# Keys and values of two kinds, projected 512 columns wide, four heads at a time

## The chip, the core and the metric

The kernel runs on one core of a Trainium2 chip. It computes one layer of a hybrid decoder, for 512 tokens of 1024 features, in one launch. The metric is the device time of an execution in microseconds (us). The engines are named as the profile names them: PE (matmul; PEld is its weight load), DVE (vector), ACT (scalar), POOL (GpSimd) and SP, whose queue issues most of the DMAs.

## What is computed

The layer is a feed-forward block, a mixer, a second feed-forward block and a gated embedding. The change is in the mixer, where one projection feeds two groups of heads. Cut to what matters here:

```python
a = rmsnorm(h, mix_norm[i])
u = a @ w_in[i]
(qa, kc, vc, ksl, vsl, kwn, vwn, ga, qf, kf, vf, fl) = jnp.split(u, split_points, axis=-1)
q_a = partial_rope(rmsnorm(split_heads(qa, N_HEADS_NSA), q_norm_nsa[i]), cos, sin)
...
k_slc = partial_rope(rmsnorm(split_heads(ksl, N_KV_NSA), k_norm_slc[i]), cos, sin)
k_win = partial_rope(rmsnorm(split_heads(kwn, N_KV_NSA), k_norm_win[i]), cos, sin)
...
o_a = nsa_attention(q_a, k_cmp, v_cmp, k_slc, split_heads(vsl, N_KV_NSA),
                    k_win, split_heads(vwn, N_KV_NSA), gates)
```

ksl, vsl, kwn and vwn are 128 columns each (two heads of 64): keys and values of the selected blocks (kind 0) and of the window (kind 1). They lie side by side in w_in, from column 768 on. Keys are normalized per head and the first 16 of their 64 features are rotated by position; values are used as they are.

## The kernel before

Tokens are handled in four tiles of 128 ("token 0" to "token 3" below, t in the code). Every float32 operand of a product is split into a part "hi" that is rounded to the matmul's type and a rest "lo", and a product is three matmuls: hi by hi, lo by hi, hi by lo (`passes`, L457). A tile of weights, 128 x 1024 numbers, is loaded on SP's queue into one of three buffers "st"; ACT copies it into one of four buffers "hi", and DVE subtracts that into one of four buffers "lo" (`split`, L373).

The stretch around the change is written in `mix` (L1068). `project` (L716) loads and splits its weights and then, for each token, issues 24 matmuls into one PSUM bank "acc" and calls `done`. First comes a projection "c" of 288 columns: the keys and values to be compressed ("T2"), gates and forget values. Then `kv_project(0)` and `kv_project(1)` (L1094), each 256 columns: for each token ACT scales the result out of PSUM into "u" (L1100), the values are split (L1102), the keys go through `head_norm` (L752: squares on ACT, a reduction on DVE, a scale and a power on POOL in `rstd`, two products on DVE), through `rope` on POOL (L742: four operations on tiles "r"), through `split_heads` (L769: a copy on ACT and a subtraction on DVE into "hl"), and PE transposes "hl" (L1109) so that copies can lay the keys into B. `q_project(0)` follows in the same manner, four heads wide.

Woven with it is the compression: `blocks` (L866) builds tiles from T2, for the keys on DVE and for the values on POOL, and `compressed` (L894) multiplies them with weights that are split tile by tile, eight matmuls a tile.

No one writes the order down. Each operation is recorded (`record`, L137) in the order in which `weave` (L197) takes the streams in turn, by the PE time that each has used. `issue` (L214) then orders all of them by a greedy rule: among the operations whose inputs are ready, on each engine, the one that by a table of costs can start first, within a window of 440 operations from the oldest that is left, and as far as the buffers of its tiles are free. Each engine executes its own list strictly in that order. So an edit at one place of the mixer moves operations up to the mixer's end.

Of the kernel before, what the change touches and what calls it, by code (L numbers as in the profile page):

```python
# [8 lines left out]
F32R = mybir.dt.float32r  # L9
AF = mybir.ActivationFunctionType  # L10
ALU = mybir.AluOpType
AX = mybir.AxisListType
PSUM = bass.MemoryType.PSUM

P = 128
# [13 lines left out]
NT = S // P  # L29
# [279 lines left out]
class Layer:  # L309
# [758 lines left out]
    def mix(self, xT, rs_in, o_nsa, o_fox, nsa_out):  # L1068
        nc = self.nc
        G, V = nc.gpsimd, nc.vector  # L1070
# [20 lines left out]
        nc.weave(self.project(xT, [(512, 256), (1280, 24), (2840, 8)], c_done, "c"))  # L1091
        B, Vt = {}, {}

        def kv_project(kind):  # L1094
            Vt[kind] = self.k4((P, 2, NT, P), F32R)
            B[kind] = [self.k4((P, 2, 512), F32R) for _ in range(2)]

            def kv_done(t, ps):
                u = self.w2()[:, :256]
                nc.scalar.mul(u, ps[:, :256], rs_in[t])  # L1100
                uv = u.rearrange("p (s h d) -> p s h d", s=2, h=2)
                self.vsplit(uv[:, 1], Vt[kind], t)  # L1102
                xn = self.w2()[:, :128].rearrange("p (h d) -> p h d", h=2)
                self.head_norm(V, uv[:, 0], xn, self.gkv[:, kind, None, :].to_broadcast([P, 2, 64]))
                self.rope(G, xn, t, 2)
                hl = self.split_heads(xn, 2, 2)
                tp = self.gub()
                for i in range(2):
                    nc.tensor.transpose(tp[:, i * P:(i + 1) * P], self.parts(hl, i, 0), self.ident)  # L1109
                k = tp[:, :256].rearrange("p (a c) -> p a c", a=2)  # L1110
                copy = nc.scalar.copy if t % 2 else V.tensor_copy
                cols = slice(t * P, (t + 1) * P)
                copy(B[kind][0][:, :, cols], k)
                copy(B[kind][1][0:64, :, cols], k[64:128])
                copy(B[kind][1][64:128, :, cols], k[0:64])
            yield from self.project(xT, [(768 + 256 * kind, 256)], kv_done, f"v{kind}")

        A = {}

        def q_project(g):  # L1120
            A[g] = [self.k4((P, 2, 512), F32R) for _ in range(2)]

            def q_done(t, ps):
                u = self.w2()[:, :256].rearrange("p (h d) -> p h d", h=4)
                nc.scalar.mul(u, ps[:, :256].rearrange("p (h d) -> p h d", h=4), rs_in[t])
                xn = self.w2()[:, :256].rearrange("p (h d) -> p h d", h=4)
                self.head_norm(V, u, xn, self.gq[:, None, :].to_broadcast([P, 4, 64]))
                self.rope(G, xn, t, 4)
                hl = self.split_heads(xn, 4, 2)
                for i in range(2):  # L1130
                    self.qT(hl, (2 * i, 2 * i + 1), A[g][i], t)
            yield from self.project(xT, [(256 * g, 256)], q_done, f"q{g}")

        def cmp_group(g):
            for t in range(NT):
                yield from self.cmp_attention(A[g], t, g, o_nsa)

        def nsa_pair(g, a):
            for kind in range(2):
                rs = self.rs_tile()  # L1140
                hd = 4 * g + 2 * a
                cols = slice(64 * hd, 64 * hd + 128)

                def write(ps, coef):
                    tmp = self.w2()
                    tv = tmp.rearrange("p (t h d) -> p t h d", t=NT, h=2)
                    V.tensor_mul(tv, ps, coef)
                    G.tensor_tensor(o_nsa[:, :, cols], o_nsa[:, :, cols],
                                    tmp.rearrange("p (t c) -> p t c", t=NT), ALU.add)
                run = lambda par: self.unit([(A[g][a][:, par], B[kind][i][:, g]) for i in range(2)], Vt[kind][:, g],  # L1150
                                            rs, par)
                yield from self.pair([run, run],
                                     rs, self.gates[:, :, hd:hd + 2, 1 + kind], write)
# [30 lines left out]
        def f_pair(p):  # L1184
# [7 lines left out]
            def write(ps, coef):  # L1192
                V.tensor_mul(o_fox[:, :, 128 * p:128 * p + 128].rearrange("p t (h d) -> p t h d", h=2), ps, coef)
            yield from self.pair([run, run], rs, None, write)

        chain = itertools.chain
        kv = kv_project(0)
        next(kv)
        wk = self.load_w1(self.d["cmp_k_w1"][0])
        blk = [self.blocks(T2[i], i) for i in range(2)]  # L1200
        cmp = chain(self.cmp_keys(blk[0], wk), self.cmp_values(blk[1], self.load_w1(self.d["cmp_v_w1"][0])),
                    self.forget_rows())
        nc.weave(chain(kv, kv_project(1), q_project(0)), cmp)
        streams = dict(c0=cmp_group(0), c1=cmp_group(1), n00=nsa_pair(0, 0), n01=nsa_pair(0, 1), n10=nsa_pair(1, 0),
                       n11=nsa_pair(1, 1), q1=q_project(1), out=nsa_out)
        for p in range(4):
# [336 lines left out]
```

## Time and profile before

| | |
|---|---|
| median of 3 runs | 1094.08 us (1092.9 to 1094.25) |
| the profiled execution | 1092.74 us |
| its span, first to last instruction | 1091.0 us |
| PE / DVE / ACT / POOL busy | 1070.5 / 768.9 / 580.0 / 192.9 us |
| granted TensorE clock, mean | 0.999 |

The profile is one execution. A busy engine is one on which an instruction runs; a matmul's end is modelled, and since matmuls are pipelined, the step from one start to the next tells more than a duration. Engine lists run in order, so an instruction that waits holds up all that stand behind it. All instructions have one line in the profile (L306, where the ordered list is emitted), and are told apart by the tiles that they write and read.

### The profile page before, as it was taken

What the parts mean: (1) busy time and instruction counts of PE and PEld (TensorE: products, weight loads), DVE (VectorE), ACT (ScalarE), POOL (GpSimd) and SP (SyncE); (2) the same over time, 40 slices, a digit from 0 to 9 for tenths busy, and PEclk for the clock granted to TensorE, in tenths of its full rate; (3) what the DMA queues carried; (4) which work ended last, traced back from release to release, by engine and by line L of the source; (5) the groups of instructions that cost most, each with busy time, mean ns of one, the idle gap of its engine ahead of it and who ended that gap; (6) DMA issues with size and microseconds to landing.
All of it is one profiled execution on the core that took longest, in us unless ns stands there. A gap on an engine that the chain in (4) does not pass through costs nothing.

```text
span 1091.0 us, 17966 instructions
## 1 busy us (share of the span) xinstructions
PE 1070.5 (98%) x6819; PEld 967.8 (89%) x6819; DVE 768.9 (70%) x1336; ACT 580.0 (53%) x1127; POOL 192.9 (18%) x338
## 2 busy tenths in 40 slices
PE   9999999999999989999999999999999999999998
PEld 6788899989997988899998888889989998899887
DVE  5976377835864777899889786977537874477473
ACT  5554155522543768888878864545414552255342
POOL 1010000000000366563344610310000000000000
PEclk9999999999999999999999999999999999999999
DMA  8486356733355521302102241677635664343431
GB/s 281 142 221 201 86 155 187 182 132 98 97 139 141 194 78 44 84 10 59 40 22 75 67 167 39 212 216 181 183 97 136 180 190 132 98 116 118 150 111 67
DMA packets 77446, 139.82 MB, mean 128 GB/s; under 512 B 13616, under 2 KB 35648, under 8 KB 77104
## 3 DMA queue, kind: packets, MB, share of 16 engines
q1 hardware_dynamic: 72400, 120.76, 34.1%
q0 software_dynamic: 4960, 17.91, 9.3%
q8 instruction: 54, 0.88, 0.3%
q14 instruction: 32, 0.26, 0.1%
HBM read 132.23 MB, written 6.42 MB: 127 GB/s over the span
## 4 chain that ended last, share of the span: by engine, by line
PE 82%; DVE 5%; POOL 3%; ACT 3%; issue 3%; DMA 3%; SPq 0%; ACTq 0%; POOLq 0%; DVEq 0%
PE acc L306 52%; PE gub L306 30%; DVE k L306 1%; DVE w L306 1%; POOL w L306 1%; POOL s L306 1%; DVE lo L306 1%; ACT w L306 1%; DMA pt<-in_quarters 1%; ACT k L306 1%; ACT hi L306 1%; POOL r L306 1%; DMA gq<-in_q_norm_nsa 1%; DMA st<-in_quarters 0%; DVE pt L306 0%
## 5 line engine op out<-in xcount | busy, mean ns | idle before, releaser
L306 PE MATMUL acc<-hi,k 128*128 128x512 f32 (+1 forms) x832 | 262.7, 389 | 2.7 <-DVE k L306 1.9
L306 ACT CAST hi<-st 128x1024 fp32r<-128x1024 f32 (+4 forms) x150 | 148.2, 991 | 181.4 <-PE acc L306 92.4
L306 DVE TENSOR_TENSOR lo<-st,hi 128x1024 fp32r<-128x1024 f32 (+4 forms) x150 | 172.9, 1155 | 64.2 <-ACT hi L306 64.1
L306 PE MATMUL acc<-hi,x 128*128 128x256 f32 (+3 forms) x784 | 203.2, 335 | 0.0
L306 PEld LDWEIGHTS acc<-hi,k 128*128 128x128 f32 x832 | 156.0, 188 | 33.9 <-issue 1.5
L306 PE MATMUL acc<-lo,k 128*128 128x512 f32 (+1 forms) x432 | 164.2, 383 | 0.2 <-DVE lo L306 0.2
L306 ACT CAST hi<-pt 128x1024 fp32r<-128x1024 f32 x68 | 71.3, 1049 | 159.1 <-PE acc L306 90.3
L306 PE MATMUL gub<-x,hi 128*128 128x256 f32 x816 | 147.4, 282 | 0.0
L306 PE MATMUL acc<-x,hi 128*128 128x256 f32 x816 | 147.3, 282 | 0.0
L306 PEld LDWEIGHTS acc<-hi,x 128*128 128x128 f32 x784 | 134.9, 189 | 8.2
L306 PE MATMUL gub<-k,hi 128*128 128x512 f32 (+1 forms) x560 | 138.3, 338 | 1.3 <-ACT hi L306 1.3
L306 DVE TENSOR_TENSOR lo<-pt,hi 128x1024 fp32r<-128x1024 f32 x68 | 83.1, 1223 | 78.8 <-ACT hi L306 78.8
L306 PE MATMUL acc<-lo,x 128*128 128x256 f32 (+3 forms) x392 | 130.8, 335 | 0.0
L306 PEld LDWEIGHTS gub<-x,hi 128*128 128x128 f32 x816 | 126.1, 189 | 0.7 <-DVE w L306 0.3
L306 PEld LDWEIGHTS acc<-x,hi 128*128 128x128 f32 x816 | 125.6, 188 | 0.0
L306 PE MATMUL gub<-x,lo 128*128 128x256 f32 x408 | 115.3, 283 | 0.0
L306 PE MATMUL acc<-x,lo 128*128 128x256 f32 x408 | 115.3, 283 | 0.0
L306 POOL DMA_DIRECT2D pt<-in_quarters x34 | 29.9, 879 | 477.4 <-DMA pt<-in_quarters 242.7
L306 PEld LDWEIGHTS gub<-k,hi 128*128 128x128 f32 x560 | 96.3, 190 | 12.9 <-ACT hi L306 1.8
L306 PE MATMUL gub<-k,lo 128*128 128x512 f32 (+1 forms) x280 | 94.5, 338 | 0.4 <-DVE lo L306 0.4
L306 PEld LDWEIGHTS acc<-lo,k 128*128 128x128 f32 (+1 forms) x432 | 79.5, 184 | 14.8 <-DVE lo L306 0.4
L306 PEld LDWEIGHTS acc<-lo,x 128*128 128x128 f32 x392 | 74.0, 189 | 4.5
(163 smaller groups left out, 1732.2 us busy)
## 6 DMA issues: line engine op xcount, KB each, us to landing
st<-in_quarters SPq DMA_DIRECT2D x51, 512.0 KB, 3.7
st<-in_ffn_wd SPq DMA_DIRECT2D x44, 512.0 KB, 5.0
pt<-in_quarters SPq DMA_DIRECT2D x34, 512.0 KB, 4.7
pt<-in_quarters POOLq DMA_DIRECT2D x34, 512.0 KB, 6.7
st<-in_quarters SPq DMA_DIRECT2D x32, 256.0 KB, 5.5
st<-in_w_in SPq DMA_DIRECT2D x48, 128.0 KB, 2.6
st<-in_first SPq DMA_DIRECT2D x16, 256.0 KB, 3.5
st<-in_w_in SPq DMA_DIRECT2D x8, 512.0 KB, 3.8
```

The source lines that it names most:

```text
L306: getattr(getattr(self.nc, op.eng), m)(*a, **k)
```

## The change

One call of `kv_project` takes the place of two. It projects 512 columns at once, so a token has one bank of 512 columns in the place of two of 256, and 24 matmuls in the place of 48. The four key heads of both kinds are squared, reduced, scaled, multiplied by their gains, rotated and split in one pass. The values are split kind by kind, and the transposes and the copies into B are made kind by kind, as before. A weight tile holds two slices of 128 rows by 512 columns where it held four by 256, so there are four tiles either way, but one token reads all four.

```diff
-        def kv_project(kind):
-            Vt[kind] = self.k4((P, 2, NT, P), F32R)
-            B[kind] = [self.k4((P, 2, 512), F32R) for _ in range(2)]
+        def kv_project():
+            for kind in range(2):
+                Vt[kind] = self.k4((P, 2, NT, P), F32R)
+                B[kind] = [self.k4((P, 2, 512), F32R) for _ in range(2)]
 
             def kv_done(t, ps):
-                u = self.w2()[:, :256]
-                nc.scalar.mul(u, ps[:, :256], rs_in[t])
-                uv = u.rearrange("p (s h d) -> p s h d", s=2, h=2)
-                self.vsplit(uv[:, 1], Vt[kind], t)
-                xn = self.w2()[:, :128].rearrange("p (h d) -> p h d", h=2)
-                self.head_norm(V, uv[:, 0], xn, self.gkv[:, kind, None, :].to_broadcast([P, 2, 64]))
-                self.rope(G, xn, t, 2)
-                hl = self.split_heads(xn, 2, 2)
-                tp = self.gub()
-                for i in range(2):
-                    nc.tensor.transpose(tp[:, i * P:(i + 1) * P], self.parts(hl, i, 0), self.ident)
-                k = tp[:, :256].rearrange("p (a c) -> p a c", a=2)
-                copy = nc.scalar.copy if t % 2 else V.tensor_copy
+                u = self.w2()
+                nc.scalar.mul(u, ps, rs_in[t])
+                uv = u.rearrange("p (a s h d) -> p a s h d", a=2, s=2, h=2)
+                for kind in range(2):
+                    self.vsplit(uv[:, kind, 1], Vt[kind], t)
+                xn = self.w2()[:, :256]
+                x4 = xn.rearrange("p (a h d) -> p a h d", a=2, h=2)
+                sq, ss = self.w2()[:, :256], self.small(4)
+                nc.scalar.activation(sq.rearrange("p (a h d) -> p a h d", a=2, h=2), uv[:, :, 0], AF.Square)
+                V.tensor_reduce(ss, sq.rearrange("p (n d) -> p n d", n=4), axis=AX.X, op=ALU.add)
+                r = self.rstd(ss, 64, 4).rearrange("p (a h) -> p a h", a=2)
+                V.tensor_tensor(x4, uv[:, :, 0], r[:, :, :, None].to_broadcast([P, 2, 2, 64]), ALU.mult)
+                V.tensor_tensor(x4, x4, self.gkv[:, :, None, :].to_broadcast([P, 2, 2, 64]), ALU.mult)
+                xn = xn.rearrange("p (n d) -> p n d", n=4)
+                self.rope(G, xn, t, 4)
+                hl = self.split_heads(xn, 4, 2)
                 cols = slice(t * P, (t + 1) * P)
...
-            yield from self.project(xT, [(768 + 256 * kind, 256)], kv_done, f"v{kind}")
+                for kind in range(2):
+                    tp = self.gub()
+                    for i in range(2):
+                        nc.tensor.transpose(tp[:, i * P:(i + 1) * P], self.parts(hl, 2 * kind + i, 0), self.ident)
...
+            yield from self.project(xT, [(768, 512)], kv_done, "v")
...
-        kv = kv_project(0)
+        kv = kv_project()
...
-        nc.weave(chain(kv, kv_project(1), q_project(0)), cmp)
+        nc.weave(chain(kv, q_project(0)), cmp)
```

The order moves with it. On DVE, around the first token's chain, before (w_630 is its "u", w_631 its normalized keys, k_618 to k_623 are the blocks and their parts):

```order
L306 TENSOR_REDUCE s_633<-w_632 128x2
L306 TENSOR_TENSOR k_618<-k_576,pos 128x16x31
L306 COPY k_577<-gub 64x2x128
L306 TENSOR_TENSOR k_618<-k_576,pos 128x16x31
L306 TENSOR_TENSOR k_619<-k_618,k_619 128x8x64
L306 TENSOR_TENSOR w_631<-w_630,s_634 128x128
L306 TENSOR_TENSOR w_631<-w_631,gkv 128x128
L306 TENSOR_TENSOR k_620<-k_618,k_620 128x8x64
```

The same place now (w_639 is token 0's "u", w_640 its normalized keys, k_627 to k_632 are the blocks and their parts, k_577 is filled just ahead):

```order
L306 TENSOR_TENSOR k_627<-k_576,pos 128x16x31
L306 TENSOR_TENSOR k_628<-k_627,k_628 128x8x64
L306 TENSOR_TENSOR k_629<-k_627,k_629 128x8x64
L306 TENSOR_TENSOR k_631<-k_630,k_631 128x8x64
L306 TENSOR_REDUCE s_642<-w_641 128x4
L306 TENSOR_TENSOR k_632<-k_630,k_632 128x8x64
L306 TENSOR_TENSOR k_607<-w_639,k_607 128x2x64
L306 TENSOR_TENSOR k_610<-w_639,k_610 128x2x64
L306 TENSOR_TENSOR w_640<-w_639,s_643 128x256
L306 TENSOR_TENSOR w_640<-w_640,gkv 128x256
```

The reduction stood ahead of the blocks' additions and now stands behind an addition and three of the four subtractions.

On ACT, from token 2's scaling on, before (w_652 is token 2's "u" of kind 0, w_662 token 3's; x_617 holds the last two of the four weight tiles of the compressed keys, the first two are copied before the first token's scaling):

```order
L306 ACTIVATE w_652<-acc,s_553 128x256
L306 CAST k_607<-w_652 128x2x64
L306 ACTIVATE w_654<-w_652 128x128
L306 CAST hi<-x_617 128x1024 x2
L306 ACTIVATE w_662<-acc,s_558 128x256
```

The same place now (w_665 is token 2's "u", x_625 and x_626 hold the four weight tiles of the compressed keys, "hi<-st" is the first tile of the queries):

```order
L306 ACTIVATE w_665<-acc,s_553 128x512
L306 CAST hl<-w_653 128x4x64
L306 CAST k_607<-w_665 128x2x64
L306 CAST k_610<-w_665 128x2x64
L306 CAST hi<-x_625 128x1024
L306 CAST k_608<-gub 128x2x128
L306 CAST k_609<-gub 64x2x128 x2
L306 ACTIVATE w_667<-w_665 128x256
L306 CAST hi<-x_625 128x1024
L306 CAST hi<-x_626 128x1024 x2
L306 CAST hi<-st 128x1024
L306 ACTIVATE w_678<-acc,s_558 128x512
```

All four tiles of the compressed keys' weights are now copied after token 2's scaling; two of them were copied before token 0's.

On PE, near the mixer's end, before (x_574 is the output of the first group of heads, "hl" is token 2 of the last projection of the forgetting heads, k_1577 and k_1578 are operands of the output projection):

```order
L306 MATMUL gub<-ident,x_574 128x128 x4
L306 MATMUL gub<-k_1488,k_1486 128x256
L306 MATMUL gub<-k_1489,k_1487 128x256
L306 MATMUL gub<-ident,x_574 128x128 x2
L306 MATMUL gub<-ident,hl 128x128 x2
L306 MATMUL acc<-hi,k_1577 128x512
L306 MATMUL acc<-lo,k_1577 128x512
```

The last of the rows between "gub<-ident,x_574" and the same "hl" now, where the six rows of 128x512 ahead of these are left out:

```order
L306 MATMUL gub<-ident,x_574 128x128 x4
L306 MATMUL acc<-hi,k_1541 128x512
L306 MATMUL gub<-ident,x_574 128x128 x2
L306 MATMUL acc<-lo,k_1541 128x512
L306 MATMUL acc<-hi,k_1542 128x512
L306 MATMUL gub<-ident,hl 128x128 x2
L306 MATMUL acc<-hi,k_1543 128x512
```

The transposes of "hl" stood ahead of the output projection's matmuls and now stand behind nine of them.

## Rows read from the trace of the kernel before

**Rows 1.** The page, part 1: busy us (share) and instructions of each engine.

```profile
PE 1070.5 (98%) x6819; PEld 967.8 (89%) x6819; DVE 768.9 (70%) x1336; ACT 580.0 (53%) x1127; POOL 192.9 (18%) x338
```

**Rows 2.** Windows: length, busy us (instructions) by engine, granted clock, DMA share, GB/s.

```profile
373.00:440.00 67.00, 60.33 (x493) 57.53 (x491) 52.65 (x133) 49.64 (x117) 42.68 (x93) 1.00 0.29 84
440.00:580.00 140.00, 138.56 (x927) 128.06 (x926) 125.77 (x385) 119.59 (x353) 60.45 (x101) 1.00 0.15 37
580.00:640.00 60.00, 56.27 (x347) 49.37 (x346) 49.59 (x134) 48.15 (x137) 29.56 (x41) 1.00 0.31 105
```

**Rows 3.** Timeline, PE: start, us, operation, tiles, shapes, count; every third matmul shown.

```profile
334.54 0.39 PE L306 MATMUL acc<-lo,k 128*128 128x512 f32 x1
...
344.74 0.39 PE L306 MATMUL acc<-lo,k 128*128 128x512 f32 x1
...
373.29 0.27 PE L306 MATMUL acc<-lo,x 128*128 128x256 f32 x1
...
376.43 0.29 PE L306 MATMUL acc<-lo,x 128*128 128x256 f32 x1
...
380.75 0.29 PE L306 MATMUL acc<-lo,x 128*128 128x256 f32 x1
```

**Rows 4.** Waits of PE, 373 to 421 us: waiter <- releaser: us, times, longest.

```profile
PE gub L306 <- DVE hl L306: 2.9, 4, 1.1
PE acc L306 <- DVE k L306: 1.3, 1, 1.3
PE gub L306 <- POOL w L306: 0.4, 1, 0.4
PE acc L306 <- DVE lo L306: 0.2, 1, 0.2
```

**Rows 5.** Groups by form, 373 to 440 us: count | busy us, mean ns | idle before.

```profile
L306 DVE TENSOR_TENSOR lo<-x,hi 128x1024 fp32r<-128x1024 f32 x8 | 9.8, 1230 | 0.6 <-ACT hi L306 0.4
L306 DVE TENSOR_TENSOR k<-k,k 128x512 fp32r<-128x512 f32 x4 | 3.8, 957 | 0.0
L306 DVE TENSOR_TENSOR hl<-w,hl 128x128 fp32r<-128x128 f32 x8 | 2.3, 291 | 5.2 <-ACT hl L306 5.1
L306 DVE TENSOR_TENSOR hl<-w,hl 128x256 fp32r<-128x256 f32 x4 | 1.6, 426 | 0.7 <-ACT hl L306 0.7
...
L306 ACT CAST hi<-x 128x1024 fp32r<-128x1024 f32 x8 | 8.3, 1046 | 0.2 <-PE acc L306 0.2
L306 ACT CAST hl<-w 128x256 fp32r<-128x256 f32 x4 | 1.5, 400 | 2.3 <-POOL w L306 2.3
...
L306 POOL TENSOR_TENSOR s<-s,mhalf 128x4 f32<-128x4 f32 x4 | 4.1, 1026 | 0.2
L306 POOL TENSOR_SCALAR s<-s 128x4 f32<-128x4 f32 x4 | 0.9, 220 | 1.8 <-DVE s L306 1.6
```

**Rows 6.** Timeline, DVE and POOL: the blocks of T2, and one rotation.

```profile
379.34 0.42 DVE L306 COPY k<-gub 64x256 f32<-64x256 f32 x1
379.79 1.03 DVE L306 TENSOR_TENSOR k<-k,pos 128x496 f32<-128x496 f32 x1
380.74 1.74 DVE L306 TENSOR_TENSOR k<-k,k 128x512 fp32r<-128x512 f32 x1
382.40 1.37 DVE L306 TENSOR_TENSOR w<-w,s 128x128 f32<-128x128 f32 x1
...
380.15 3.46 POOL L306 TENSOR_TENSOR k<-k,pos 128x496 f32<-128x496 f32 x2
...
428.68 0.32 POOL L306 TENSOR_TENSOR r<-w,cos 128x64 f32<-128x64 f32 x1 [1.10 <-DVE w L306]
428.96 0.46 POOL L306 TENSOR_TENSOR r<-w,sin 128x32 f32<-128x32 f32 x2
```

**Rows 7.** Timeline, PE, 620 to 625 us: the two that waited.

```profile
621.66 0.44 PE L306 MATMUL gub<-ident,x 128*128 128x128 f32 x2 [0.90 <-DVE s L306]
623.50 0.44 PE L306 MATMUL gub<-ident,hl 128*128 128x128 f32 x2 [1.40 <-DVE hl L306]
```

More of the change, by code (lines that the diff above doesn't have):

```diff
@@ L1092, in mix @@
         B, Vt = {}, {}
-        def kv_project(kind):
-            Vt[kind] = self.k4((P, 2, NT, P), F32R)
-            B[kind] = [self.k4((P, 2, 512), F32R) for _ in range(2)]
+        def kv_project():
+            for kind in range(2):
+                Vt[kind] = self.k4((P, 2, NT, P), F32R)
+                B[kind] = [self.k4((P, 2, 512), F32R) for _ in range(2)]
             def kv_done(t, ps):
-                u = self.w2()[:, :256]
-                nc.scalar.mul(u, ps[:, :256], rs_in[t])
-                uv = u.rearrange("p (s h d) -> p s h d", s=2, h=2)
-                self.vsplit(uv[:, 1], Vt[kind], t)
-                xn = self.w2()[:, :128].rearrange("p (h d) -> p h d", h=2)
-                self.head_norm(V, uv[:, 0], xn, self.gkv[:, kind, None, :].to_broadcast([P, 2, 64]))
-                self.rope(G, xn, t, 2)
-                hl = self.split_heads(xn, 2, 2)
-                tp = self.gub()
-                for i in range(2):
-                    nc.tensor.transpose(tp[:, i * P:(i + 1) * P], self.parts(hl, i, 0), self.ident)
-                k = tp[:, :256].rearrange("p (a c) -> p a c", a=2)
-                copy = nc.scalar.copy if t % 2 else V.tensor_copy
-                cols = slice(t * P, (t + 1) * P)
-                copy(B[kind][0][:, :, cols], k)
-                copy(B[kind][1][0:64, :, cols], k[64:128])
-                copy(B[kind][1][64:128, :, cols], k[0:64])
-            yield from self.project(xT, [(768 + 256 * kind, 256)], kv_done, f"v{kind}")
@@ new lines, in kv_done @@
+                cols = slice(t * P, (t + 1) * P)
+                for kind in range(2):
+                    tp = self.gub()
+                    for i in range(2):
+                        nc.tensor.transpose(tp[:, i * P:(i + 1) * P], self.parts(hl, 2 * kind + i, 0), self.ident)
+                    k = tp[:, :256].rearrange("p (a c) -> p a c", a=2)
+                    copy = nc.scalar.copy if (t + kind) % 2 else V.tensor_copy
+                    copy(B[kind][0][:, :, cols], k)
+                    copy(B[kind][1][0:64, :, cols], k[64:128])
+                    copy(B[kind][1][64:128, :, cols], k[0:64])
```

## The prediction

> **What bounds the kernel now.** I read the page first: the span is 1091.0 us and PE is busy for 98% of it, DVE for 70%, ACT for 53%, POOL for 18% [rows 1]. The profiled execution took 1092.74 us, so 1.74 us lie outside the span; the median of the three runs is 1094.08 us, 1.34 us above the profiled one. I form the sum on the profiled execution and carry its result over to the median.
>
> The windows by stage come next [rows 2]. [...] The change touches the second window, 373 to 440 us: PE is idle there for 67.00 - 60.33 = 6.67 us, a third of all its idle time. From 440 to 580 us it is idle for 1.44 us in 140, and from 580 to 640 us for 3.73 us. The reader should see that DVE is at 90% from 440 to 580 us and yet PE hardly waits: PE's own work is the bound there, and the others are cover that just suffices. So an edit counts by two things alone: what it takes from PE's work, and what it does to PE's waits.
>
> Third, PE's timeline gives the step from one matmul to the next [rows 3]: 45 matmuls of 512 columns in 344.74 - 334.54 = 10.20 us are 0.2267 us each; 36 of 256 columns in 380.75 - 376.43 = 4.32 us are 0.1200 us each. Fourth, PE's waits up to the last transposes of this projection [rows 4]: 2.9 + 1.3 + 0.4 + 0.2 = 4.8 us. The largest group, four waits of together 2.9 us, is the transposes of a token waiting for "hl", the end of the chain of normalization and rotation.
>
> **The change part by part.** *Matmuls.* Two kinds x 4 tokens x 24 matmuls of 256 columns become 4 x 24 of 512: 192 x 0.1200 - 96 x 0.2267 = 23.04 - 21.76 = 1.28 us less. They stand on the engine that bounds, so I take -1.28 us. [...]
>
> *The waits of the chains.* Eight chains of two heads become four of four heads, and each is longer. The 128x256 forms of the chain stand in the same window, from the query projection [rows 5]: the last subtraction takes 0.43 us (0.29 for two heads), the copy before it 0.40, the power on POOL 1.03. I take 0.43 us for the reduction and each of the two products too, which have the same shape on the same engine. The scaling of 512 columns out of PSUM has no row in this stage; it lies between the copies of 256 (0.40) and 1024 columns (1.05 [rows 5]), some 0.6 us, and beside other work for token 0. What matters is the work the order puts on PE over each chain.
>
> Token 0: the projection starts at about 373.17 us (its second matmul is at 373.29 [rows 3]); 24 x 0.2267 = 5.44 us, four transposes of "c" (0.4) and the wait of 0.4 us for their input, which stays [rows 4], end its matmuls at 379.4. The new order has 35 matmuls between them and its transposes, so PE arrives at 379.4 + 35 x 0.2267 = 387.3 us. The chain is bound elsewhere: in DVE's new order its reduction stands behind all work on the blocks but one piece. That starts when the last copy ahead of it ends, 379.76 us [rows 6]: one addition (1.03 [rows 6]), three subtractions (0.96 each [rows 5]) and the reduction (0.43) reach 384.1; scale and power on POOL (0.22 + 1.03 [rows 5]), the two products (0.86), the rotation on POOL (0.32 + 0.46 + 0.32 [rows 6]; the addition taken as long as the first product), copy and subtraction (0.40 + 0.43) reach 388.1, and eight hand-overs, estimated at 0.05 us each, 388.6. PE waits 1.3 us; between 0.8 (the copy 0.5 us earlier, since no reduction stands among the blocks' work any more) and 2.1 (1.3 + 1.74 - 0.96, one more subtraction held up by POOL, next).
>
> POOL's additions are slow company: while two of them take 3.46 us, a 128x512 subtraction of DVE takes 1.74 us where the mean is 0.96, and a 128x128 product 1.37 us [rows 5, 6]. [...]
>
> Tokens 1 to 3: token 1 has 33 wide matmuls over its chain and both transposes of token 0, and I find no wait. Token 2 has 24 wide ones, the 32 of the compressed keys and 28 of the queries, 24 x 0.2267 + 60 x 0.12 = 12.6 us, against a chain of about 6 us by the steps above, but on ACT and DVE its copy and its product stand behind the splits below: 1.2 us, between 0 and 1.7. Token 3: 0.3.
>
> *The splits of the compressing weights.* This is what the change costs. "hi" and "lo" have four buffers. The projection now needs four weight tiles for one token and holds all four until its last token has read them; before, two of the four "hi" copies of the compressed keys' weights ran in the first token's time. In the new order all four, and the first of the queries' weights, stand after token 2's scaling on ACT. Token 1's transposes come at 388.6 + 0.4 + 22 x 0.2267 = 394.0 us, the first tile is copied then (1.05 [rows 5]), and from about 395 us on DVE has five subtractions of 1.23 us [rows 5], three copies (3 x 0.42 [rows 6] = 1.3), a reduction and a product in a row: 5 x 1.23 + 1.3 + 0.43 + 0.43 = 8.3 us. PE has 15 wide matmuls and the 32 of the compressed keys for that time, 3.4 + 3.8 = 7.2 us. With 0.3 us by which DVE starts later and 0.6 in which it waits for a buffer to come free I take 2.0 us of waits, between 1.4 and 2.6. The waits of 1.3 and 0.2 us that belong to these matmuls now [rows 4] go.
>
> Together: 0.4 + 1.3 + 1.2 + 0.3 + 2.0 = 5.2 us in the place of 4.8, so +0.4; the ends are 0.4 + 0.8 + 1.4 = 2.6 (-2.2) and 0.4 + 2.1 + 1.7 + 0.3 + 2.6 = 7.1 (+2.3).
>
> *The rest of the mixer.* The planner orders everything anew up to the end of the mixer, about 640 us. One place can be priced: token 2 of the last forgetting projection now makes PE wait 1.40 us for its "hl" [rows 7]. In the new order nine matmuls of 512 columns, 2.0 us, stand ahead of these transposes, so that wait is covered. The 0.90 us just before it [rows 7] stands between the same rows in both orders and stays. Since the same reordering can open a wait of this size at any of the other chains, I count half of it, -0.7, between -1.4 and +1.0.
>
> *At no price.* The four loads of weight tiles stay four, and no load is among PE's releasers [rows 4]. The copies into B, the transposes, the table loads and the banks are the same in number or fewer.
>
> Sum: -1.28 + 0.4 - 0.7 = -1.6 us. 1092.74 - 1.6 = 1091.1 for a profiled execution, and 1094.08 - 1.6 = **1092.5 us** for the median. Its own range, with the terms half way to their ends, is 1091.0 to 1094.5 us.
>
> **The rivals.** *A, the chains are covered.* Half as many chains run through POOL and DVE, so both are freer than before and no chain is late: the low end of the waits and all of the 1.40: -1.28 - 2.2 - 1.4 = -4.9, 1089.2 us. For it: 2.9 us of today's waits are on "hl". Against it: token 0's reduction stands behind the blocks' work.
>
> *B, slower: the splits become the bound.* If each of the four tiles shows its copy and its subtraction (1.05 + 1.23 us [rows 5]) against the eight matmuls of 0.12 us that read it, PE waits 4 x (2.28 - 0.96) = 5.3 us instead of 2.0, and with tokens 0, 2 and 3 at their upper ends the waits are 0.4 + 2.1 + 1.7 + 0.3 + 5.3 = 9.8, +5.0; with the matmuls' -1.28 that is +3.7, 1097.8 us. It turns into a loss beyond what can be told from no change once the waits up to the last transposes pass 4.8 + 1.28 + 2.2 = 8.3 us. For it: these tiles wait for buffers that the wide projection holds. Against it: wide matmuls stand between the tiles' uses.
>
> *C, the freed vector work counts.* If DVE set the pace from 440 us on, each of 16 pairs of 128x128 instructions that becomes one of 128x256 gives 2 x 0.291 - 0.426 = 0.16 us [rows 5], 2.5 us, beside the matmuls: -3.8, 1090.3 us. For it: DVE's 90%. Against it: PE's 1.44 us of idle time in 140.
>
> **How the numbers follow.** About 0.2%, 2.2 us, is what a measurement of this kernel can tell from no change. My forecast, a gain too small for that, gets 0.44; A 0.27 and C 0.07 are faster by more; B 0.22 is slower by more. The range reaches to A's 1089.2 and B's 1097.8 with a little off the far end: 1088.8 to 1097.4 us. [...]
>
> **What would show it.** In the profile after: 96 matmuls of 512 columns of this projection with a step of 0.227 us; waits of PE on "hl" at token 0 of about 1.3 us and none at token 1; PE held by "lo" among the compressing matmuls between 395 and 405 us for about 2 us; busy time of PE lower by about 1.3 us; no wait at the nine wide matmuls of the last projection. Wrong would be: waits in this stage above 8 us (B) or below 3 us (A), or a wait of over 2 us at a chain that I did not look at, between 440 and 640 us.

## The result, and the profile after

The changed kernel takes 1085.95 us (median; 1085.05 to 1086.81), the kernel before 1094.11 us timed beside it: a ratio of 0.993, interval 0.9919 to 0.9942, so 8.2 us less. The prediction was 1092.5 us, between 1088.8 and 1097.4; it is wrong in the size and in the case that it held likeliest.

The page of the kernel after, part 1 (as [rows 1]):

```profile
PE 1068.3 (98%) x6723; PEld 963.0 (89%) x6723; DVE 767.7 (71%) x1320; ACT 579.4 (53%) x1115; POOL 183.6 (17%) x314
```

The span is 1085.0 us, 6.0 less. This profile reaches the mixer 1.2 us later than that of before, and is as much behind already at 75 us, where nothing has changed (in the profiles of this study the last matmul of "c" starts anywhere between 371.4 and 375.5 us). So 7.2 us were gained from there on, and the windows that answer to [rows 2] are moved by 1.2 us (columns as there):

```profile
374.20:441.20 67.00, 61.81 (x413) 54.23 (x412) 54.81 (x132) 50.94 (x120) 37.59 (x73) 1.00 0.30 86
441.20:581.20 140.00, 139.39 (x938) 130.27 (x937) 125.72 (x379) 120.20 (x348) 62.59 (x102) 1.00 0.16 39
581.20:641.20 60.00, 58.27 (x359) 51.46 (x358) 52.54 (x136) 50.17 (x136) 23.40 (x36) 1.00 0.33 115
```

PE is idle for 5.19, 0.61 and 1.73 us, where it was 6.67, 1.44 and 3.73. More than half of the idle time that went lies in the two later windows, where no line of the program was edited.

For the comparisons below I lay the lists of matmuls side by side by the work in them. A matmul of N columns counts 0.4167 N + 13.5 ns, an estimate laid through the two steps of [rows 3]: 226.7 - 120.0 = 106.7 ns for 256 columns more, and some 13 ns beside. At 128 columns or fewer it counts 60 ns, a choice of mine that no row shows (two of 128 columns take 0.38 us at 595.15 us where one takes 0.27 at 597.61, so a second one adds 0.11; timeline of the kernel before, PE); both kernels have the same 720 of these. What PE takes beyond this count is lost. "Stage" is the loss from the last matmuls of "c" to about 479 us, "later" from there to about 658 us, both against the kernel before. In this account the changed kernel has 1.3 us less work, loses 2.1 us less in the stage and 3.6 us less later: 7.0 of the 7.2 us. After 658 us the two lose the same. Since the lists differ in order, the split depends on where it is drawn: at 470, 500 or 520 us in the place of 479 the changed kernel's stage reads -2.4, -1.7 and -2.3, so it is good to some 0.4 us. And it is an account of one profiled execution a kernel, where the ratios below are of all executions.

### The profile page after: what moved, and what is told of

Read it like the earlier page. It is cut to its first block, busy times and chain, and to the rows that moved or that the text cites. A ratio compares the mean times of both kernels' runs of the same rounds, so it can differ in the third digit from the quotient of the medians.

```text
span 1085.0 us, 17692 instructions
## 1 busy us (share of the span) xinstructions
PE 1068.3 (98%) x6723; PEld 963.0 (89%) x6723; DVE 767.7 (71%) x1320; ACT 579.4 (53%) x1115; POOL 183.6 (17%) x314
## 4 chain that ended last, share of the span: by engine, by line
PE 82%; DVE 6%; ACT 3%; DMA 3%; POOL 3%; issue 3%; SPq 0%; ACTq 0%; POOLq 0%; DVEq 0%
PE acc L306 52%; PE gub L306 30%; DVE k L306 2%; DVE lo L306 2%; POOL s L306 1%; ACT k L306 1%; DVE w L306 1%; ACT w L306 1%; DMA pt<-in_quarters 1%; DMA k<-in_x 1%; POOL r L306 1%; DMA gq<-in_q_norm_nsa 1%; POOL w L306 1%; ACT hi L306 1%; DVE pt L306 0%
## 5 line engine op out<-in xcount | busy, mean ns | idle before, releaser
L306 PE MATMUL acc<-hi,x 128*128 128x384 f32 (+3 forms) x720 | 199.4, 349 | 0.3 <-ACT hi L306 0.3
L306 PEld LDWEIGHTS acc<-hi,x 128*128 128x128 f32 x720 | 127.1, 189 | 11.1 <-ACT hi L306 0.4
L306 PE MATMUL acc<-lo,x 128*128 128x384 f32 (+3 forms) x360 | 125.1, 348 | 1.7 <-DVE lo L306 1.7
L306 PEld LDWEIGHTS gub<-k,hi 128*128 128x128 f32 x560 | 96.3, 189 | 12.6 <-ACT hi L306 1.6
L306 PEld LDWEIGHTS gub<-x,lo 128*128 128x128 f32 x408 | 76.9, 188 | 0.0
```

Source lines behind the costliest of these rows:

```text
L306: getattr(getattr(self.nc, op.eng), m)(*a, **k)
```

## The experiments

Three theories stood at the start. "Fewer chains": four long chains in the place of eight are what helps. "Width": the wide matmuls are. "Order": the edit makes the planner order the rest of the mixer anew, and that order happens to be a better one. Each ratio is to the kernel before, timed on the same chip beside it; "work", "stage" and "later" are us against the kernel before, less is faster.

| kernel | work | stage | later | ratio |
|---|---|---|---|---|
| changed | -1.3 | -2.1 | -3.6 | 0.9930 |
| e1, wide bank, eight chains | -1.3 | +5.1 | -3.2 | 1.0003 |
| e2, narrow banks, four chains | 0 | -2.6 | -1.5 | 0.9968 |
| e3, before, all delays 204 ns | 0 | -0.5 | -2.9 | 0.9965 |
| e5, changed, later order of before | -1.3 | +2.1 | +1.0 | 1.0013 |
| e6, before, later order of changed | 0 | +3.6 | -3.7 | 0.9988 |

### One part of the change alone

*e1*: the bank is 512 wide, but each kind has its own scaling, norm, rotation and "hl", as before.

```diff
             def kv_done(t, ps):
+                for kind in range(2):
+                    u = self.w2()[:, :256]
+                    nc.scalar.mul(u, ps[:, 256 * kind:256 * kind + 256], rs_in[t])
...
             yield from self.project(xT, [(768, 512)], kv_done, "v")
```

> The change's projection of 512 columns, but each kind keeps its own chain of two heads (eight chains, as before). Theory 'fewer chains' (the gain of 8.2 us is 1.3 us of matmul work and the rest is that four chains take the place of eight): 1.3 us below before, some 1092.8 us, with PE's waits on hl back near the 7.0 us of before. Theory 'order' (the rest is where the planner's new order happens to put PE's waits): 1.3 us below before and then anything from -6 to +3 us, with waits at other places than before. Theory 'width' (the wide projection itself gives the gain): 1086 us.

Measured: 1093.96 us, 1.0003 (0.9992 to 1.0014): no gain. PE's largest wait of the mixer is here (timeline of e1, PE; waits in brackets):

```profile
406.34 0.58 PE L306 MATMUL acc<-lo,x 128*128 128x256 f32 x1 [3.01 <-DVE lo L306]
...
409.15 0.41 PE L306 MATMUL acc<-lo,x 128*128 128x256 f32 x1
409.36 0.63 PE L306 MATMUL acc<-hi,x 128*128 128x256 f32 x2
409.79 0.63 PE L306 MATMUL acc<-lo,x 128*128 128x256 f32 x2
```

The "lo" that it waits for is the split of the queries' first tile. Timeline of e1, DVE:

```profile
402.73 0.29 DVE L306 TENSOR_TENSOR w<-w,s 128x128 f32<-128x128 f32 x1 [0.59 <-POOL s L306]
...
404.01 0.29 DVE L306 TENSOR_TENSOR w<-w,s 128x128 f32<-128x128 f32 x1 [0.59 <-POOL s L306]
...
405.08 1.21 DVE L306 TENSOR_TENSOR lo<-st,hi 128x1024 fp32r<-128x1024 f32 x1
```

Its "hi" was copied on ACT at 399.50 us, in 1.05 us; but the split stands in DVE's list behind the products of two chains, each of which waits 0.59 us for POOL's power. And behind the wait PE is slower: from 409.15 to 409.79 us three matmuls of 256 columns take 0.64 us, 0.213 us each where [rows 3] has 0.1200. The last section has the granted clock of that stretch. Wide matmuls with the old chains thus come near the slower rival of the prediction, "the splits become the bound", but by another path: PE waits 0.30 and 0.34 us at the tiles of the compressed keys that B priced, and 3.01 us at the queries' first tile, whose split stands on DVE behind rows that wait for POOL.

*e2*: the reverse. Each 512-wide matmul is issued as two of 256 into the halves of the bank; chains of four heads as in the changed kernel.

```diff
-                    nc.tensor.matmul(ps[:, :n], lhsT=a[:, t * P:(t + 1) * P], rhs=b,
...
+                    for c in ((0, 256), (256, 512)) if n == 512 else ((0, n),):
+                        nc.tensor.matmul(ps[:, c[0]:c[1]], lhsT=a[:, t * P:(t + 1) * P], rhs=b[:, c[0]:c[1]],
```

> The change's chains of four heads, but the projection's matmuls are 256 columns wide again, in two halves of the bank (192 matmuls). 'Fewer chains': 1.3 us above the changed kernel, some 1087.3 us, waits on hl as few as there. 'Order': 1.3 us above the changed kernel and then several us to either side. 'Width': 1094 us.

Measured: 1088.92 us, 0.9968 (0.9955 to 0.9981). The stage gains 2.6 us with no matmul saved; with the wide matmuls work and stage together gain 3.4, so the width adds some 0.8 us, and in e1, without the merged chains, it gained nothing. In these runs the merged chains carry the stage. But each run has one order of the stage, made anew by the planner, so this is shown for those orders and not for others.

### The order of the later part

*e3* and *e4* change nothing but one entry of the planner's table of delays, from PE to the other engines, in the kernel before and in the changed one:

```diff
-    LAT = {"tensor": dict(vector=197.0, scalar=197.0, gpsimd=197.0, sync=197.0, tensor=0.0),
+    LAT = {"tensor": dict(vector=204.0, scalar=204.0, gpsimd=204.0, sync=204.0, tensor=0.0),
```

> The kernel before, with one number of the planner's table nudged: the delay from PE to the others 204 in the place of 197 ns. The same operations, another order from the middle of the mixer on. 'Fewer chains': within 1.5 us of before, 1092.6 to 1095.6 us, since the eight chains are what it is. 'Order': off by 2 us or more to either side.

> The changed kernel with the same nudge. 'Fewer chains': within 1.5 us of the changed kernel, 1084.5 to 1087.5 us. 'Order': off by 2 us or more, most likely upward, since the changed kernel's order is then a lucky one.

Measured: the kernel before gets 3.3 us faster (1089.49, 0.9965, 0.9952 to 0.9978), the changed one slower (1087.98, 0.9954, 0.994 to 0.9969, where it was 0.9930: some 2.6 us). A number that computes nothing moves the time by more than the change was forecast to.

*e5* and *e6* exchange the later orders. The 2395 operations recorded behind the stage are the same in both kernels. LATE holds, for each engine, the order that they have in the other kernel, and the planner may only follow it:

```diff
+                    if op.i in late:
+                        if op.i != fixed[e][-1]:
+                            continue
+                    elif op.i > oldest + WINDOW:
+                        continue
```

> The changed kernel, but the 2395 operations that are recorded behind the weave of keys, values, first queries and compression (from about 440 us on) are issued on each engine in exactly the order that they have in the kernel before; the stage of the change keeps its own order. Theory 'order': what was gained from 440 us on (about 4 us in the two profiles: idle time 2.44 us at 440 to 640, the rest in steps) was luck of the planner's new order and goes with it; the stage's part, about -1.3 of matmuls and -1.5 of waits, stays: 1093 - 2.8 = about 1090 us, with the waits of 0.90 (on s) and 1.40 us (on hl) back near 620 us. Theory 'fewer chains': the gain comes from the chains of four and does not hang on the later order: about 1085.5 us.

> The reverse: the kernel before up to about 440 us, and from there on each engine in the order of the changed kernel. Theory 'order': the later part gains by itself, without any change of the computation: 1093 - 4 = about 1089 us, and no wait of over 1 us at 585 to 625. Theory 'fewer chains': no gain, 1093 us.

Measured: 1094.12 us, 1.0013 (1.0 to 1.0026), and 1092.05 us, 0.9988 (0.9978 to 0.9998). Taken whole, both miss what "order" expected, and e5 is far from the 1085.5 us of "fewer chains". The stage column tells why: where a stage meets a later order that was made for another one, PE waits once for long, 3.62 us in e5 and 2.04 us in e6 (timelines of e5 and e6, PE):

```profile
429.09 0.91 PE L429 MATMUL gub<-ident,hl 128*128 128x128 f32 x4 [3.62 <-DVE w L429]
```

```profile
443.91 0.48 PE L429 MATMUL gub<-ident,cs 128*128 128x128 f32 x1 [2.04 <-POOL cs L429]
```

Behind that seam the expectation holds: the changed kernel's later order loses 3.7 us less in the kernel *before*, as it does in its own (3.6), and the later order of before gives the changed kernel nothing. Its two waits of [rows 7] are back, to the hundredth (timeline of e5, PE):

```profile
624.92 0.44 PE L429 MATMUL gub<-ident,x 128*128 128x128 f32 x2 [0.90 <-DVE s L429]
626.76 0.44 PE L429 MATMUL gub<-ident,hl 128*128 128x128 f32 x2 [1.40 <-DVE hl L429]
```

So the later 3.6 us hang on the order and not on fewer or longer operations. (That e5 loses 1.0 us more there goes with a lower clock behind these two waits; the last section has its row.)

*How good are other orders?* The next runs nudge the same delay for the later operations alone, so that the stage keeps its order (e4 differs from such a kernel by three rows of PE's list, and stands for 204 ns on the changed side):

```diff
+        nc.LAT = dict(Plan.LAT, tensor=dict(vector=230.0, scalar=230.0, gpsimd=230.0, sync=230.0, tensor=0.0))
```

> The kernel before with a nudge of the planner's table for the later operations alone (those recorded behind the weave of the stage): the delay from PE to the other engines 230 ns where it was 197. Nothing else. Theory 'order': the later part of before was an unlucky draw and nearly any other order is better, so 1 to 4 us less, 1089 to 1092 us. Theory 'fewer chains': within 1 us of 1093.

> The changed kernel with the same nudge for the later operations alone. Theory 'order': the later part of the changed kernel was a lucky draw, so 1 to 3 us more than it, 1087 to 1089 us. Theory 'fewer chains': within 1 us of 1086.

> The kernel before, the planner's delay from PE to the other engines 211 ns where it was 197, for the operations recorded behind the stage alone. A second draw of the later part's order. Theory 'order': as the first draw (230 ns, -4.2 us), 1088.5 to 1091 us. If the first draw was lucky: 1092 to 1094.

> The changed kernel with the same nudge for the later operations alone. Theory 'order': between the changed kernel and the two nudged ones, 1086 to 1088.5 us, so that the mean of the changed kernel's draws lies 2 to 3.5 us below the mean of the draws of the kernel before (the matmuls' 1.3 and the stage's 2 us).

> The kernel before, delay from PE to the other engines 204 ns for the operations recorded behind the stage alone (the run with 204 for all operations changed the stage too). With the runs at 211 and 230 ns the later part lost 3.3 and 3.9 us less than in the kernel before. Theory 'order' (before's own draw was a poor one): again 2 to 4 us less, 1089 to 1091 us. Theory 'the change': those two were lucky, about 1093 us.

> The same with 220 ns. Theory 'order': 1089 to 1091 us. Theory 'the change': about 1093 us.

> The changed kernel with 220 ns for the later operations. Theory 'order': the stage's -2.1 and the matmuls' -1.3 stay, the later part lands among the other draws (0.8 to 3.6 us less than in the kernel before): 1086 to 1089 us, more than the changed kernel itself if a wait of over 2 us brings the clock down. Theory 'the change': the later part gains 3.6 us again, 1086 us or less.

| delay | before: us, ratio (interval), stage, later | changed: us, ratio (interval), stage, later |
|---|---|---|
| 197 (the two kernels) | 1, 0, 0 | 1085.95, 0.9930 (0.9919 to 0.9942), -2.1, -3.6 |
| 204 (e13, e4) | 1092.69, 0.9993 (0.9983 to 1.0003), 0.0, -0.4 | 1087.98, 0.9954 (0.994 to 0.9969), -2.0, -1.3 |
| 211 (e11, e12) | 1088.76, 0.9961 (0.9948 to 0.9973), -0.1, -3.2 | 1088.35, 0.9961 (0.9948 to 0.9974), -2.0, -0.7 |
| 220 (e14, e15) | 1092.41, 0.9992 (0.9982 to 1.0003), +0.5, -0.5 | 1088.41, 0.9959 (0.9944 to 0.9974), -1.9, -1.0 |
| 230 (e7, e8) | 1088.52, 0.9962 (0.9945 to 0.998), +0.2, -3.9 | 1087.75, 0.9954 (0.9939 to 0.997), -2.0, -0.9 |

Four of the five draws of the changed kernel lie between 0.9954 and 0.9961, and the changed kernel as it stands is the best of them. The kernel before has two draws 0.4% below and three near 1: e7, e8, e11, e12 and e15 came where "order" expected them, but e13 and e14 missed its 1089 to 1091 us, so the kernel before's own draw is a common one, not a freak. No gain of the later part by the change is seen: the means of its five draws are -1.6 (before) and -1.5 us (changed), with a standard error of the difference of 1.0. The stage of the changed kernel, one and the same order in all five, gains 1.9 to 2.1 us. The mean ratios are 0.9982 and 0.9952: the change by itself is worth 0.0030, 3.3 us, with a standard error of some 1.1 from the spread of the draws. That is as much as the matmuls' 1.3 and the stage's 2.0. Of the other 4.9 of the 8.2 us the account puts 3.6 down to the draw of the later part. The last 1.3 it can't place; they are within what the ratio's interval leaves open (6.3 to 8.9 us). (Without the two kernels themselves the means of four differ by 0.0020, 2.2 us.)

### Moving PE's list alone

*e9*, from the kernel before: matmuls that stand behind the waits at 621 to 623 us go ahead of them; DVE, ACT and POOL keep their lists. (The six matmuls of the other move stand ahead of the transposes of "hl" at 595.15 us, which had not waited, and not of those at 585.10. So the wait there, 0.95 us in e9, was not tried, and of the 2.3 us expected 1.4 were left to be tested.)

```diff
+L306 MATMUL acc<-hi,k_1577 128x512
+L306 MATMUL acc<-lo,k_1577 128x512
...
 L306 MATMUL gub<-ident,x_574 128x128 x2
 L306 MATMUL gub<-ident,hl 128x128 x2
-L306 MATMUL acc<-hi,k_1577 128x512
-L306 MATMUL acc<-lo,k_1577 128x512
```

> The kernel before with only PE's own list changed, at two places; DVE, ACT and POOL keep their lists row for row. Six matmuls of 384 columns are put ahead of the four transposes of hl that waited 0.99 us at 585.10, and six of 512 columns of the output projection ahead of the transposes that waited 0.90 us (on s, 621.66) and 1.40 us (on hl, 623.50). Theory 'order': those waits are only PE's arrival a little too early, so 6 x 0.18 = 1.1 and 6 x 0.2267 = 1.36 us of work cover 0.99 and 1.36 of them: about -2.3 us, 1090.5 us. If the vector engines were the bound there (fewer vector operations being what helped the changed kernel), the waits move to the next transposes and the time stays within 0.7 us of 1092.7.

Measured: 1095.77 us, 1.0026 (1.0015 to 1.0038), slower; no theory expected that. Timeline of e9, PE:

```profile
623.42 0.79 PE L575 MATMUL acc<-hi,k 128*128 128x512 f32 x1 [3.15 <-ACT k L575]
624.02 0.63 PE L575 MATMUL acc<-lo,k 128*128 128x512 f32 x1
624.44 1.05 PE L575 MATMUL acc<-hi,k 128*128 128x512 f32 x2
625.30 0.63 PE L575 MATMUL acc<-lo,k 128*128 128x512 f32 x1
```

And ACT there:

```profile
622.12 0.41 ACT L575 CAST hl<-w 128x256 fp32r<-128x256 f32 x1 [1.78 <-POOL w L575]
...
623.02 0.35 ACT L575 CAST k<-gub 128x256 fp32r<-128x256 f32 x1
```

The matmuls put ahead need "k", whose copy stands in ACT's list behind the copy of "hl", and that waits 1.78 us for POOL. One waiting row on ACT holds up both things that PE could do. In the changed kernel three copies "k<-gub" stand ahead of the next copy of "hl" on ACT: the whole place was ordered otherwise, and PE's row order, which the prediction looked at, is only a part of that.

*e10*, from the changed kernel: six wide matmuls of token 2 go ahead of token 0's transposes, and one matmul ahead of the transposes at 619.33 us.

> The changed kernel with only PE's own list changed: six of the 512-wide matmuls of token 2 are put ahead of token 0's four transposes, which waited 1.11 us on hl at 390.24, and one matmul ahead of the transposes that waited 0.69 us at 619.33. All other engines keep their lists. Theory 'order': the wait is token 0's chain (about 10 us from the bank's end to its hl) against too little work of PE, so 1.36 us of work ahead cover it: -1.1 and -0.2, 1084.7 us. If the chain itself were the bound of the stage, the wait shows again at token 1's transposes: 1086 us.

Measured: 1084.31 us, 0.9932 (0.9915 to 0.9949), the same as the changed kernel's 0.9930. Timeline of e10, PE:

```profile
393.11 0.66 PE L600 MATMUL gub<-ident,hl 128*128 128x128 f32 x4 [0.48 <-DVE hl L600]
...
402.79 0.39 PE L600 MATMUL acc<-lo,x 128*128 128x256 f32 x1 [1.26 <-DVE lo L600]
...
406.50 0.63 PE L600 MATMUL gub<-ident,hl 128*128 128x128 f32 x4 [0.23 <-DVE hl L600]
```

Of token 0's 1.11 us 0.63 are covered, but PE then meets the queries' split 0.17 us earlier and token 2's "hl" 0.23 us earlier. About 0.2 of 0.6 us are left. The wait of 0.69 us at 619.33 became one of 0.59 us at the matmul that was put ahead. The 1084.31 us are near the 1084.7 that were expected, but the ratio shows no gain over the changed kernel.

## Why the prediction was wrong, step by step

Two steps failed. The term for the rest of the mixer, -0.7 us with ends of -1.4 and +1.0, took the planner's new order at one place for the whole of it: the later part alone measured -3.6, and other orders of the same program move it by as much. And the sum of the stage's waits, +0.4 us, charged the same lateness of DVE twice: it measured -1.6.

*What bounds the kernel*: right. PE's work and its waits are the whole account, at clock 1.00 in the windows of both profiles.

*Matmuls, -1.28*: right in sign, too large. Timeline of the kernel after, PE, the wide projection:

```profile
377.59 0.39 PE L306 MATMUL acc<-lo,x 128*128 128x512 f32 x1
...
388.73 0.40 PE L306 MATMUL acc<-lo,x 128*128 128x512 f32 x1
```

These are 48 matmuls apart, 0.2321 us each and not the 0.2267 that I took over from another stage. With this step the term is 23.04 - 96 x 0.2321 = 0.76 us less; the other 0.5 us of the account's 1.3 stand among the stage's loss.

*Waits up to the last transposes, 4.8 to 5.2*: they went to 0.42 + 1.11 + 1.09 + 0.55 = 3.2 (timeline of the kernel after, PE; the wait of 0.42 us is that of the transposes of "c"):

```profile
390.24 0.66 PE L306 MATMUL gub<-ident,hl 128*128 128x128 f32 x4 [1.11 <-DVE hl L306]
...
405.25 0.39 PE L306 MATMUL acc<-lo,x 128*128 128x256 f32 x1 [1.09 <-DVE lo L306]
...
408.77 0.63 PE L306 MATMUL gub<-ident,hl 128*128 128x128 f32 x4
...
412.80 0.45 PE L306 MATMUL acc<-lo,k 128*64 128x256 f32 x2 [0.55 <-DVE lo L306]
```

Token 0 waited 1.11 us (1.3 said), token 1 not at all (said), "c" 0.42 us (0.4 said). The 1.11 is right in part by luck: the three subtractions beside POOL's additions took 4.04 us and not 2.88, which the blocks' work made good by starting some 0.9 us earlier, counted from the end of "c". The hand-overs, put at 0.05 us each with no row behind them, are there: the nine gaps from the reduction's end to the last subtraction add up to 0.43 us. The splits cost 1.64 us (2.0 said, between 1.4 and 2.6), but not where they were priced: the tiles of the compressed keys, between 395 and 405 us, made PE wait nowhere; 1.09 us came at the queries' first tile and 0.55 at the first of the compressed values. The step that failed is the sum. Tokens 2 and 3 were to cost 1.2 + 0.3, for which the prediction shows no working (it found 12.6 us of cover for a chain of 6), and cost nothing. Timeline of the kernel after, DVE:

```profile
403.64 0.42 DVE L306 TENSOR_TENSOR w<-w,s 128x256 f32<-128x256 f32 x1 [0.91 <-POOL s L306]
403.98 1.22 DVE L306 TENSOR_TENSOR lo<-st,hi 128x1024 fp32r<-128x1024 f32 x1
...
408.19 0.42 DVE L306 TENSOR_TENSOR hl<-w,hl 128x256 fp32r<-128x256 f32 x1 [0.32 <-ACT hl L306]
```

Token 2's "hl" is done at 408.61 and PE comes at 408.77. Without the 1.09 us that it had waited for the split it would, with DVE as late, have come at 407.68 and waited 0.93. The same lateness of DVE was priced twice, once at the split and once at the chain behind it. PE pays it once, at whichever comes first; e10 shows the same from the other side. Ahead of both, DVE's list stands still for 0.91 us for POOL.

Behind the last transposes, up to 479 us, the stage gained another 1.0 us (the rest of its 3.4), where the prediction priced nothing. The kernel before waits there for the queries' "hl" (its timeline, PE); in the changed kernel two shorter waits, 0.63 us at 425.28 and 0.65 at 439.69, take its place:

```profile
425.94 0.63 PE L306 MATMUL gub<-ident,hl 128*128 128x128 f32 x4 [1.46 <-DVE hl L306]
```

*The rest of the mixer, -0.7 (between -1.4 and +1.0)*: about -3.6 and outside its ends. The 1.40 us went, as said. The 0.90 us "stays", I wrote, because the rows around it on PE are the same; it went too. It is released by DVE, and I compared PE's lists alone. A third wait, which I had not looked at, went as well (timeline of the kernel before, PE):

```profile
585.10 0.66 PE L306 MATMUL gub<-ident,hl 128*128 128x128 f32 x4 [0.99 <-DVE hl L306]
```

Two waits came instead, both among the nine wide matmuls that were to wait for nothing (timeline of the kernel after, PE):

```profile
617.01 0.50 PE L306 MATMUL acc<-hi,k 128*128 128x512 f32 x1 [0.57 <-ACT k L306]
...
619.33 0.41 PE L306 MATMUL gub<-ident,w 128*128 128x128 f32 x2 [0.69 <-DVE k L306]
```

From 0.99 + 0.90 + 1.40 = 3.29 to 0.57 + 0.69 = 1.26 us, these waits are 2.0 of the 3.6 us; the rest is in shorter ones that I have not followed. The larger error is the range: one place was priced, and the ends were set by that place, while the draws of the same program spread over 3.9 us (before) and 2.9 us (changed) in this part. The result lies 2.85 us below the low end, as much as the changed kernel's spread. (The sum's own range, too, is a little off: its terms half way to their ends give 1090.9 to 1094.3, not 1091.0 to 1094.5.)

*The rivals*: A, "the chains are covered", had the right side and the right mechanism for tokens 2 and 3; that its 1089.2 us is near the changed kernel's other draws is luck, since it priced no draw. B is near e1's stage, not the changed kernel's. C, the freed vector work, has nothing for it: with the same later order the two kernels lose the same there (e6).

Not settled: why the 512-wide step is 0.2321 us in this projection, and whether another order of the stage would keep the 2.0 us, since all five draws of the changed kernel share one. The only others with merged chains are e2's (2.6 us) and the moved list of e10 (2.2 us); in e3 the stage of the kernel before has another order, and gains 0.5 us without the change.

## What to carry to other kernels

Where a planner orders the program, time a few neutral nudges of its table before and after an edit: the spread of the draws (here 0.4%, where the edit was worth 0.3) is the yardstick, and a single pair of timings measures the draw as much as the edit. Do not add up along the list the waits that one late engine causes: here PE waited 1.09 us at the queries' split, and token 2's "hl", which would else have held it for 0.93 us, then held it for none. And look at the lists of ACT and DVE, not only PE's: a row that waits for POOL with a split or a copy behind it is where PE's 3.01 us in e1 and 3.15 us in e9 were made.

## What the runs showed of the hardware

A wait of PE can be followed by a lower clock. In e9 the matmuls behind the wait of 3.15 us take 0.43 us, where this shape takes 0.2267 [rows 3]. Windows of e9 (columns as in [rows 2]):

```profile
620.00:624.00 4.00, 0.85 (x4) 0.57 (x3) 2.74 (x10) 2.21 (x9) 2.89 (x5) 0.76 0.64 162
624.00:628.00 4.00, 4.00 (x13) 2.87 (x11) 0.76 (x3) 1.12 (x3) 2.23 (x3) 0.50 1.03 409
628.00:632.00 4.00, 3.71 (x21) 2.86 (x21) 3.77 (x11) 3.86 (x11) 0.00 (x0) 0.88 0.84 316
```

The granted clock is 0.50 in the middle one. In e1 it is 0.72 over the 12 us from the wait on:

```profile
404.00:416.00 12.00, 9.63 (x56) 9.20 (x56) 8.92 (x24) 5.97 (x13) 9.36 (x25) 0.72 0.61 178
```

It fell likewise at the seams of e5 and e6 (waits of 3.62 and 2.04 us, lowest window of 4 us at 0.66 and 0.50), in e13 and e14 (1.84 and 2.05 us, 0.74 and 0.62), and in e4 and e8 (2.34 and 2.32 us, 0.78 in both), here e8's wait and windows:

```profile
617.12 0.44 PE L306 MATMUL gub<-ident,hl 128*128 128x128 f32 x2 [2.32 <-DVE hl L306]
```

```profile
616.00:620.00 4.00, 2.88 (x11) 2.13 (x12) 3.36 (x10) 3.06 (x10) 2.81 (x6) 0.78 0.71 225
620.00:624.00 4.00, 4.00 (x20) 3.25 (x20) 3.00 (x9) 3.32 (x10) 0.81 (x1) 0.80 1.00 393
```

The length of the wait alone does not decide. In e2 PE waited longer, 2.51 us, and kept its clock:

```profile
619.21 0.44 PE L306 MATMUL gub<-ident,hl 128*128 128x128 f32 x2 [2.51 <-DVE hl L306]
```

```profile
616.00:620.00 4.00, 1.49 (x10) 1.05 (x9) 2.92 (x9) 2.15 (x7) 2.95 (x4) 1.00 0.51 145
620.00:624.00 4.00, 4.00 (x23) 3.17 (x22) 4.00 (x11) 3.57 (x12) 2.70 (x3) 1.00 0.90 310
```

And the pair of 0.90 and 1.40 us left the clock at 1.00 in the kernel before, but in e5 the same pair was followed by 0.66:

```profile
628.00:632.00 4.00, 4.00 (x17) 3.03 (x16) 3.09 (x8) 3.06 (x9) 3.34 (x3) 0.66 1.04 420
```

The executions of one kernel differ in this too: of the 79 timings of the kernel before that stand beside the runs, twelve have a mean granted clock of 0.997 and took 1095.4 us in the mean, and six have 1.0 and took 1092.4 us. What decides whether a wait is followed by a lower clock, no run here shows.

In the account above these stretches are inside the "stage" and "later" columns: for e8, by an estimate from its two windows, (1 - 0.78 + 1 - 0.80) x 4.00 = 1.7 us, most of what parts its later -0.9 from the changed kernel's -3.6 in the profiled execution. It is not shown that this parts their medians: two of e8's executions have a mean clock of 1.0 and took 1087.22 and 1087.91 us, two have 0.998 and took 1087.49 and 1087.59.

In the mixer's stretch from 370 to 660 us nine of the profiles have a wait of PE of 1.84 us or more; behind eight of them the clock fell, and behind e2's it did not. So such a wait should be priced with a second term, as a chance.
